# Expert weights as plain float32, two half arrays for up to 64 tokens, and a longer ring of loads

## The chip, the cores and the metric

One core of one Trainium2 chip runs the kernel. The metric is the device time of one execution in microseconds (us), the median of several runs. In what follows PE is the matrix engine, DVE VectorE, ACT ScalarE, POOL GpSimd, and SP the engine whose queue issues the loads of weights.

## The reference

Two decoder layers over 256 tokens of 1024 channels. Each layer has a mixer (sparse attention, a convolution and a state space layer), then a feed-forward part, then a gate with a per-layer embedding, each followed by a layer norm. The feed-forward part of the first layer is dense; that of the second is the one which this change touches:

```python
def moe_swiglu(x, router, w1, w3, w2):
    logits = (x @ router).astype(jnp.float32)
    top_vals, top_idx = lax.top_k(logits, TOP_K)
    wts = jax.nn.softmax(top_vals, axis=-1)
    comb = jnp.einsum('blk,blke->ble', wts, jax.nn.one_hot(top_idx, N_EXPERTS, dtype=jnp.float32))
    y = jnp.zeros(x.shape, jnp.float32)
    for e in range(N_EXPERTS):
        y = y + comb[..., e:e + 1] * swiglu(x, w1[e], w3[e], w2[e])
    return y.astype(x.dtype)
```

There are 8 experts, each token goes to 2 of them, and an expert's weights are 1024x3584 (w1 and w3) and 3584x1024 (w2) in float32: 44 MB an expert, 352 MB in all. With the inputs that the reference draws, the experts get 64, 20, 68, 41, 119, 126, 13 and 61 tokens.

## The kernel before, in words

The layers run one after the other. In the expert stage (`moe`) the experts go in order, 0 to 7. For every pair of experts `gather` takes the tokens' rows by a product with a one-hot matrix (`Dm`, token by slot) into x transposed, 128 slots an expert. `expert` then streams the weights in 42 loads of 1 MB: 28 of w1 and w3 by chunks of 1024, 1024, 1024 and 512 columns (of each chunk first w1's 4 loads, or 2 in the last, then w3's), 14 of w2. The products of w1 and w3 with x (`mgu`, two PSUM banks each) go through SwiGLU into `hb`, `hb` is transposed by PE (`hT`) into `ht`, and `ht` times w2 gives `mo`. `mo` goes back to the tokens by a product with the one-hot matrix transposed (`sc`, the scatter), and DVE adds it to the running sum.

No product is made in plain float32. Every load is split: ACT rounds it to the float32r format (`whi`, line 308) and DVE forms the rest (`wlo`, line 309), in pieces of 128x1024; x and `ht` are split alike. `mm3` (lines 303 to 305) then makes three products for each row of 128 weights and each half of 512 columns: x high times w high, x low times w high, x high times w low.

The loads go into a ring of places (`self.ring`, `load`): 12 for each round, and two more beside them in the first one. SP issues them in order; a load waits until the place's former contents have been split. Two first loads of expert 0 are split ahead (`EARLY`, `ready`). The order of the work on each engine is that of the code as the scheduler of the language lays it out, with `after` holding an instruction behind another one.

An expert may have more than 128 tokens. For that, ahead of expert 6 (`OVF`) all engines read the largest count, and a branch (`tc.If`, line 1457) leads to a second pass or over it; with these inputs it leads over it. The next loads of expert 6 are issued before it, into the places that the second pass doesn't use.

At the end of the last expert the last rows of w2 go by half (`held`), the norm follows, and then the gate's weights, which are loaded through the same ring (four loads of 1 MB).

Of the kernel before, what the change touches and what calls it, by code (L numbers as in the profile page):

```python
# [15 lines left out]
P = 128  # L16
# [14 lines left out]
# columns of the constant table  # L31
# [8 lines left out]
# columns of the per-layer parameter table  # L40
# [10 lines left out]
def const_table():  # L51
    """Constants that depend on shapes alone."""
# [19 lines left out]
def square_consts():  # L72
    """Identity, causal mask, strict order, ones, column numbers."""
    import numpy as np

    r = np.arange(P)
    c = (np.eye(P), np.where(r[None, :] <= r[:, None], 0.0, NEG), (r[:, None] < r[None, :]) * 1.0, np.ones((P, P)), np.broadcast_to(r, (P, P)))
    return np.concatenate(c, 1).astype(np.float32)


def param_table(a):
    """The small parameters of each layer side by side, one row per partition; only moved, never computed on."""
# [3 lines left out]
    for l in range(DEPTH):  # L86
        put = lambda n, v: t[l].__setitem__((slice(None), slice(_L[n], _L[n] + v.shape[1])), v)
        col = lambda v: v.reshape(-1, P).T
        # S5: partition (r, n) of tile j is state n of group 2 j + r
# [19 lines left out]
        w2 = a["cmp_w2"][l].reshape(2, 2, P, 64).transpose(0, 2, 1, 3)  # [j, p, c, d]  # L109
# [7 lines left out]
def lay_out(a):  # L117
    """Arrays in the order in which the kernel reads them."""
# [31 lines left out]
# GpSimd's share: row tiles of a square weight, score tiles that it scales and S5 products, by layer  # L150
# [3 lines left out]
RB = 4  # loads of weights in flight  # L154
RBN = 2  # more of them beside the experts
OV = 2  # the last of them, the overflow's
HB = 4  # split weights in flight
SPARE = ("h1", "h2")  # tiles that take a load before their first use
EARLY = 2  # loads of the first expert split ahead
# [16 lines left out]
GT0 = ("o", "y", "bu", "s")  # L176


# [10 lines left out]
class Trunk:  # L189
    def __init__(self, ctx, tc, a, out):  # L190
# [8 lines left out]
        self.spare = []  # room for loads once the ring is full for the first time  # L199
        self.pre = []  # weights loaded ahead  # L200
        self.ready = []  # weights split ahead
# [12 lines left out]
    def psum(self, name, **tags):  # L214
        """PSUM of a phase: buffers of each kind of tile, acc of two banks, one and tr of one."""
# [27 lines left out]
    def load(self, src, a, b):  # L243
        """DRAM view [128, a, b] -> SBUF."""
        if self.spare and self.nload == self.full:
            pool, tag, n = self.spare.pop(0)
        else:
            pool, tag, n = self.ring[self.nload % len(self.ring)]
            self.nload += 1
        raw = pool.tile([P, 2048], F32, tag=tag, name="wraw", bufs=n)[:, : a * b]  # L250
        v = raw.rearrange("p (a b) -> p a b", a=a)
        self.loaded = self.nc.sync.dma_start(v, src)
        return v

    def parts(self, raw, a, b, low=None):
        """(index, hi, lo) of the a rows of a loaded weight, split into float32r parts; low: the engine of the low parts."""
        nc = self.nc
        step = max(1, 1024 // b)
        for i0 in range(0, a, step):
# [3 lines left out]
            hi = self.st.tile([P, 1024], F32R, tag="hi", name="whi", bufs=HB)[:, :n]  # L263
            lo = self.st.tile([P, 1024], F32R, tag="lo", name="wlo", bufs=HB)[:, :n]
# [5 lines left out]
    def stream(self, src, a, b):  # L270
        if self.ready:
            yield from self.ready.pop(0)
        else:
# [1335 lines left out]
```

## Time and profile before

| | |
|---|---|
| median of 3 runs | 1678.53 us (1678.34 to 1679.22) |
| span of the profiled execution | 1677.6 us, 0.9 below the median |
| busy: PE, DVE, ACT, POOL | 93%, 84%, 66%, 16% |
| moved by DMA | 445.21 MB, mean 265 GB/s |
| expert loads | 336 of 1024 KB |
| expert stage, first to last product | 622.7 to 1628.1 us |

A busy share is that of the whole span, over stages with different limits. PEclk in a row of windows is the clock that PE was granted, as a share of full speed. A timeline row gives the start, the time to the end of the last of its instructions, and how many they are; in brackets stands the idle time before it and who ended it.

### The profile page before, as it was taken

What the parts mean: (1) busy time and instruction counts of PE and PEld (TensorE: products, weight loads), DVE (VectorE), ACT (ScalarE), POOL (GpSimd) and SP (SyncE); (2) the same over time, 40 slices, a digit from 0 to 9 for tenths busy, and PEclk for the clock granted to TensorE, in tenths of its full rate; (3) what the DMA queues carried; (4) which work ended last, traced back from release to release, by engine and by line L of the source; (5) the groups of instructions that cost most, each with busy time, mean ns of one, the idle gap of its engine ahead of it and who ended that gap; (6) DMA issues with size and microseconds to landing.
All of it is one profiled execution on the core that took longest, in us unless ns stands there. A gap on an engine that the chain in (4) does not pass through costs nothing.

```text
span 1677.6 us, 20721 instructions
## 1 busy us (share of the span) xinstructions
PE 1552.2 (93%) x7390; PEld 1235.8 (74%) x7391; DVE 1407.4 (84%) x1635; ACT 1100.2 (66%) x1413; POOL 276.2 (16%) x209
## 2 busy tenths in 40 slices
PE   6676999998988779999999999999999979999997
PEld 6444787886855578878888778778778768878875
DVE  7998567648789679999988988988988978999988
ACT  6355554434655438878877777777777757877874
POOL 5754108303145240000000000000000000010022
PEclk9898999999978779999999999999999989999998
DMA  7421565554540368999989989989989869999941
GB/s 265 151 101 38 196 201 176 176 181 146 178 176 1 137 265 314 361 352 370 361 314 361 360 335 365 356 309 368 349 340 368 331 252 391 384 377 340 365 155 51
DMA packets 139632, 445.21 MB, mean 265 GB/s; under 512 B 7408, under 2 KB 19312, under 8 KB 138496
## 3 DMA queue, kind: packets, MB, share of 16 engines
q1 hardware_dynamic: 138496, 437.42, 71.0%
q0 software_dynamic: 1024, 6.38, 1.0%
q8 instruction: 60, 0.98, 0.2%
q14 instruction: 52, 0.43, 0.1%
HBM read 442.72 MB, written 1.05 MB: 265 GB/s over the span
## 4 chain that ended last, share of the span: by engine, by line
PE 61%; DVE 4%; issue 1%; DMA 1%; ACT 0%; SPq 0%; POOL 0%; DVEq 0%; POOLq 0%; ACTq 0%
PE mgu L305 12%; PE mgu L303 12%; PE mgu L304 12%; PE mo L303 6%; PE mo L304 6%; PE mo L305 6%; PE hT L1405 1%; PE xe L1373 1%; DVE wlo L309 1%; DMA wraw<-in_moe_w_dram 1%; DVE x L526 1%; DVE x L1443 1%; DVE x L527 0%; PE wo L303 0%; PE wo L304 0%
## 5 line engine op out<-in xcount | busy, mean ns | idle before, releaser
L309 DVE TENSOR_TENSOR wlo<-wraw,whi 128x1024 fp32r<-128x1024 f32 (+2 forms) x774 | 930.9, 1231 | 134.5 <-ACT whi L308 101.2
L308 ACT ACTIVATE whi<-wraw 128x1024 fp32r<-128x1024 f32 (+2 forms) x781 | 805.7, 1052 | 257.8 <-PE mgu L304 79.1
L304 PE MATMUL mgu<-whi,xl 128*128 128x512 f32 x896 | 352.6, 394 | 0.0
L303 PE MATMUL mgu<-whi,xh 128*128 128x512 f32 x896 | 352.4, 394 | 0.0
L305 PE MATMUL mgu<-wlo,xh 128*128 128x512 f32 x896 | 339.8, 396 | 5.1 <-DVE wlo L309 5.1
L305 PEld LDWEIGHTS mgu<-wlo,xh 128*128 128x128 f32 x896 | 167.4, 188 | 47.2 <-DVE wlo L309 12.3
L304 PEld LDWEIGHTS mgu<-whi,xl 128*128 128x128 f32 x896 | 168.4, 188 | 36.3 <-DVE xl L309 0.2
L303 PEld LDWEIGHTS mgu<-whi,xh 128*128 128x128 f32 x896 | 168.2, 188 | 35.0
L303 PE MATMUL mo<-whi,ht 128*128 128x512 f32 x448 | 175.9, 393 | 0.0
L304 PE MATMUL mo<-whi,ht 128*128 128x512 f32 x448 | 175.4, 392 | 0.0
L305 PE MATMUL mo<-wlo,ht 128*128 128x512 f32 x448 | 158.2, 392 | 0.1
L505 POOL DMA_DIRECT2D lnp<-in_lnp_dram x5 | 2.8, 567 | 795.9 <-ACT xh L308 766.4
L305 PEld LDWEIGHTS mo<-wlo,ht 128*128 128x128 f32 x448 | 83.8, 188 | 18.9 <-DVE wlo L309 0.5
L304 PEld LDWEIGHTS mo<-whi,ht 128*128 128x128 f32 x448 | 84.1, 188 | 18.2
L303 PEld LDWEIGHTS mo<-whi,ht 128*128 128x128 f32 x448 | 84.2, 188 | 17.7 <-ACT whi L308 0.2
L304 PE MATMUL fffn_w<-whi,xl 128*128 128x512 f32 (+1 forms) x192 | 72.0, 375 | 0.0
L303 PE MATMUL fffn_w<-whi,xh 128*128 128x512 f32 (+1 forms) x192 | 71.7, 373 | 0.0
L305 PE MATMUL fffn_w<-wlo,xh 128*128 128x512 f32 (+1 forms) x192 | 71.5, 372 | 0.0
L308 ACT ACTIVATE ht<-hT 128x512 fp32r<-128x512 f32 x56 | 33.5, 598 | 49.6 <-PE hT L1405 49.5
L1402 DVE TENSOR_TENSOR hb<-hb,mgu 128x512 f32<-128x512 f32 x56 | 38.3, 683 | 25.6 <-PE mgu L305 25.6
L950 DVE SCALAR_TENSOR_TENSOR cy<-upad,pk,cy 128x256 f32<-128x256 f32 x60 | 52.8, 879 | 1.2
L1401 ACT ACTIVATE hb<-mgu 128x512 f32<-128x512 f32 x56 | 33.1, 590 | 13.7 <-PE mgu L305 13.7
(374 smaller groups left out, 2314.0 us busy)
## 6 DMA issues: line engine op xcount, KB each, us to landing
wraw<-in_moe_w_dram SPq DMA_DIRECT2D x336, 1024.0 KB, 5.9
wraw<-in_ffn_w_dram SPq DMA_DIRECT2D x33, 1024.0 KB, 5.1
wraw<-in_cmp_w_dram SPq DMA_DIRECT2D x8, 1024.0 KB, 5.5
wraw<-in_w_out_dram SPq DMA_DIRECT2D x8, 1024.0 KB, 7.6
wraw<-in_ple_gate_w_dram SPq DMA_DIRECT2D x8, 1024.0 KB, 4.9
wraw<-in_w_in_dram SPq DMA_DIRECT2D x8, 792.0 KB, 6.2
wraw<-in_w_in_dram SPq DMA_DIRECT2D x8, 768.0 KB, 8.2
lnp<-in_lnp_dram POOLq DMA_DIRECT2D x5, 1024.0 KB, 4.9
```

Of the source, the lines that this page charges most:

```text
L303: mm(dst, xh, wh, start=start, stop=False)
L304: mm(dst, xl, wh, start=False, stop=False)
L305: return mm(dst, xh, wl, start=False, stop=stop)
L308: h = self.hi = self.nc.scalar.activation(dh, src, AF.Copy)
L309: return h, (low or self.nc.vector).tensor_tensor(dl, src, dh.bitcast(F32), op=ALU.subtract)
L526: nc.vector.scalar_tensor_tensor(out[:, c], r[:, c], mv[:, 0:1], lnp[:, 0, c], op0=ALU.subtract, op1=ALU.mult)
L950: nc.vector.scalar_tensor_tensor(y0, u(0, k), w(0, k), y0, op0=ALU.mult, op1=ALU.add)
L1373: self.gmm = self.nc.tensor.matmul(ps[:, at : at + n], src[:, tt, k * P : (k + 1) * P], Dm[tt], start=first, stop=last)
L1401: nc.scalar.activation(hb, accs[0][h], AF.Silu)
L1402: self.gated = nc.vector.tensor_mul(hb, hb, accs[1][h])
L1405: nc.tensor.transpose(ps[:, i * P : (i + 1) * P], hb[:, i * P : (i + 1) * P], self.ident)
L1443: nc.vector.scalar_tensor_tensor(y[:, tt, hs], sc[h], comb[tt], y[:, tt, hs], op0=ALU.mult, op1=ALU.add)
```

## The change

In the expert stage the weights go to PE as they land, as float32 moving operands, with no split; x and the hidden tile are float32 too. Each row of weights takes two products, one for each half of the columns, in place of six. `either` makes two versions of each group of two loads (`GRP`), 8 products of 512 columns or 16 of 256, and PE picks one by the expert's count, which it reads into a register: with more than 64 tokens (`SM`) the two products go one after the other over the full array (128 slots); with up to 64, the stationary operand has 64 columns, and the two halves of the weights' columns go to the two halves of the array's columns (rows 0 to 63 and 64 to 127 of PSUM, in two banks). The rows of a bank that such a product doesn't write are zeroed first (`pair`, DVE). A second one-hot matrix (`D2`) has the slots 64 further for experts with few tokens, for the scatter of the second half.

The transposes of the hidden tile, of the one-hot matrices and the scatter are put off behind the next group of products (`todo`, `flush`); the gather of the next pair goes into w2's products of the expert before it (`ahead`), but for expert 6, where it follows the overflow. The ring takes in the places of the split weights (`hl`, now one tile for both parts) and of x's low part (`xl`), and one more (`mp`'s); outside of the expert stage the weights are still split. Ahead of the overflow 16 loads of expert 6 are issued. `held`, the last rows by half, is gone. The overflow's second pass uses the full array and has no branch in it.

```diff
@@ the ring, in rest and moe
             if l % 2:
                 self.ring = [(rb, "raw", RBN)] * RBN + [(self.st, "raw", RB)] * RB + [(self.xp, "pp", 1), (ra, "raw", 1)]
-                self.ring += [(re, "raw", 2)] * 2 + [(rd, "raw", OV)] * OV
+                self.ring += [(self.st, "hl", HB)] * HB + [(self.cp, "xl", 1)]
+                self.ring += [(re, "raw", 2)] * 2
...
+                self.over = (rd, "raw", OV)
+                self.ring += [self.over] * OV
...
+        self.ring.append((mp, "raw", 1))
+        self.pre = [self.load(*s) for s in self.expert_loads(j, 0)[:EARLY]]
@@ gather
                 if k % 2 and tt == TORD[1]:
-                    ks = slice(k - 1, k + 1)
-                    self.split(self.xh[:, ks, :n], self.xl[:, ks, :n], ps[:, : 2 * n].rearrange("p (k s) -> p k s", k=2))
+                    v = ps[:, : 2 * n].rearrange("p (k s) -> p k s", k=2)
+                    if k % 4 == 1:
+                        nc.scalar.activation(xe[:, k - 1 : k + 1, :n], v, AF.Copy)
+                    else:
+                        nc.vector.tensor_copy(xe[:, k - 1 : k + 1, :n], v)
@@ expert
+    def either(self, n, emit):
+        if n is None:
+            emit(False)
+        else:
+            with self.tc.If(n > SM) as many:
+                emit(False)
+            with many.Else():
+                emit(True)
+        self.flush()
...
+        rows = (slice(0, SM), slice(P - SM, P))
+        def pair(name):
+            acc = self.pair(name)
+            if n is not None:
+                for h in range(2):
+                    nc.vector.memset(acc[h][rows[1 - h]], 0.0)
+            return acc
...
-                    for kk, wh, wl in self.stream(w[wi][:, u * ku : (u + 1) * ku, c0 : c0 + cw], ku, cw):
-                        k = u * ku + kk
-                        for h in range(cw // 512):
-                            hs = slice(h * 512, (h + 1) * 512)
-                            self.mm3(acc[h], xeh[:, k], xel[:, k], wh[:, hs], wl[:, hs], k == 0, k == KT - 1)
+                    ws = get()
+                    def emit(few):
+                        for u, w in enumerate(ws):
+                            for i in range(ku):
+                                k = (u0 + u) * ku + i
+                                for h in range(2):
+                                    wk = w[:, i, h * hw : (h + 1) * hw]
+                                    dst, x = (acc[h][rows[h], :hw], xe[:, k, 0:SM]) if few else (acc[h][:, :hw], xe[:, k])
+                                    mm(dst, x, wk, start=k == 0, stop=k == KT - 1)
+                    self.either(n, emit)
...
+            self.todo.append(lambda ci=ci, hw=hw, hbs=hbs: turn(ci, hw, hbs))
```

On PE, where the first expert passes from w1 and w3 to w2, the rows before are these (`hT` are transposes, `ht` the hidden tile's parts; the number behind a name tells a tile from the next of its kind):

```order
L305 MATMUL mgu_5558<-wlo_5595,xh_4565 128x512
L303 MATMUL mo_5615<-whi_5619,ht_5084 128x512
L304 MATMUL mo_5615<-whi_5619,ht_5084 128x512
L305 MATMUL mo_5615<-wlo_5620,ht_5084 128x512
L303 MATMUL mo_5616<-whi_5619,ht_5084 128x512
L304 MATMUL mo_5616<-whi_5619,ht_5084 128x512
L305 MATMUL mo_5616<-wlo_5620,ht_5084 128x512
L303 MATMUL mo_5615<-whi_5629,ht_5084 128x512
L1405 MATMUL hT_5608<-sqr_104,hb_5605 128x128 x4
L304 MATMUL mo_5615<-whi_5629,ht_5084 128x512
```

At the same place now, with a pair of branches around each group:

```order
L1444 MATMUL hT<-sqr,hb 128x128 x8
L1412 COMPARE_AND_BRANCH
L1468 MATMUL mgu<-wraw,xe 128x256 x16
L1412 UNCONDITIONAL_BRANCH
L1468 MATMUL mgu<-wraw,xe 64x256 x16
L1412 UNCONDITIONAL_BRANCH
L1444 MATMUL hT<-sqr,hb 128x128 x2
L1412 COMPARE_AND_BRANCH
L1503 MATMUL mo<-wraw,ht 128x512 x8
L1412 UNCONDITIONAL_BRANCH
L1503 MATMUL mo<-wraw,ht 64x512 x8
L1412 UNCONDITIONAL_BRANCH
```

One group of two loads has 24 products before, and has 8 now, in two versions of which one runs; the transposes stand between groups.

On DVE, in the later half of the first expert, before (`wlo` are the low parts of the weights):

```order
L1402 TENSOR_TENSOR hb_5291<-hb_5291,mgu_5200 128x512
L309 TENSOR_TENSOR wlo_5338<-wraw_5335,whi_5337 128x1024
L309 TENSOR_TENSOR wlo_5348<-wraw_5335,whi_5347 128x1024
L309 TENSOR_TENSOR ht_5290<-hT_5294,ht_5290 128x512
L1402 TENSOR_TENSOR hb_5301<-hb_5301,mgu_5201 128x512
L309 TENSOR_TENSOR wlo_5360<-wraw_5357,whi_5359 128x1024
L309 TENSOR_TENSOR wlo_5370<-wraw_5357,whi_5369 128x1024
L309 TENSOR_TENSOR ht_5290<-hT_5304,ht_5290 128x512
L309 TENSOR_TENSOR wlo_5382<-wraw_5379,whi_5381 128x1024
L309 TENSOR_TENSOR wlo_5392<-wraw_5379,whi_5391 128x1024
```

In the same stretch now (`mgu` and `mo` memsets zero the rows of the other half; the branches are jumps to the join that PE's branch needs):

```order
L1476 TENSOR_TENSOR hb<-hb,mgu 128x512
L1412 UNCONDITIONAL_BRANCH
L1476 TENSOR_TENSOR hb<-hb,mgu 128x512
L1432 MEMSET mo 64x512 x2
L1447 COPY ht<-hT 128x512
L1432 MEMSET mgu 64x512
L1412 UNCONDITIONAL_BRANCH
L1432 MEMSET mgu 64x512
L1476 TENSOR_TENSOR hb<-hb,mgu 128x256 x2
L1412 UNCONDITIONAL_BRANCH
L1447 COPY ht<-hT 128x256
L1412 UNCONDITIONAL_BRANCH x7
```

The splits are gone; memsets, copies and unconditional branches stand in their place.

## Rows read from the trace of the kernel before

**Rows 1.** Page, parts 1 (busy us and share) and 4 (the last chain).
```profile
PE 1552.2 (93%) x7390; PEld 1235.8 (74%) x7391; DVE 1407.4 (84%) x1635; ACT 1100.2 (66%) x1413; POOL 276.2 (16%) x209
...
PE 61%; DVE 4%; issue 1%; DMA 1%; ACT 0%; SPq 0%; POOL 0%; DVEq 0%; POOLq 0%; ACTq 0%
```

**Rows 2.** Timeline of PE: start us, us, engine, line, operation.
```profile
699.36 0.39 PE L304 MATMUL mgu<-whi,xl 128*128 128x512 f32 x1
...
700.73 0.39 PE L304 MATMUL mgu<-whi,xl 128*128 128x512 f32 x1
```

**Rows 3.** Timeline: first product of experts 0, 2, 3, 6; last one.
```profile
622.74 0.48 PE L303 MATMUL mgu<-whi,xh 128*128 128x512 f32 x1
...
870.03 0.62 PE L303 MATMUL mgu<-whi,xh 128*128 128x512 f32 x2
...
992.57 0.40 PE L303 MATMUL mgu<-whi,xh 128*128 128x512 f32 x1
...
1386.92 0.63 PE L303 MATMUL mgu<-whi,xh 128*128 128x512 f32 x2
...
1628.12 0.39 PE L305 MATMUL mo<-wlo,ht 128*128 128x512 f32 x1
```

**Rows 4.** Groups by form, 650 to 1600 us: busy us, mean ns.
```profile
L309 DVE TENSOR_TENSOR wlo<-wraw,whi 128x1024 fp32r<-128x1024 f32 x634 | 754.7, 1223 | 48.2 <-ACT whi L308 17.7
```

**Rows 5.** Waits of the load queue, 700 to 1360: us, times, longest.
```profile
SPq L252 <- DVE wlo L309: 550.9, 211, 16.2
```

**Rows 6.** Windows: busy of PE, PEld, DVE, ACT, POOL; PEclk, share, GB/s.
```profile
600.00:610.00 10.00, 2.83 (x21) 2.37 (x19) 9.72 (x8) 2.19 (x4) 8.82 (x4) 0.68 1.01 403
700.00:740.00 40.00, 40.00 (x178) 32.73 (x178) 36.19 (x32) 31.18 (x31) 0.00 (x0) 1.00 1.00 377
1390.00:1440.00 50.00, 50.00 (x229) 40.86 (x228) 46.52 (x44) 40.77 (x45) 0.00 (x0) 1.00 1.03 404
```

**Rows 7.** Timeline of PE: float32 products of 512 columns, full array.
```profile
95.84 1.02 PE L903 MATMUL s<-kTz,qT 128*128 128x512 f32 x2
...
98.66 0.59 PE L903 MATMUL s<-kTz,qT 128*128 128x512 f32 x1
...
L903 PE MATMUL s<-kTz,qT 128*128 128x512 f32 x32 | 19.5, 699 | 2.6 <-ACT kTz L705 2.6
```

**Rows 8.** Timeline of PE: float32 products on two halves of the array.
```profile
529.42 1.09 PE L927 MATMUL o<-pT,vv 128*64 128x128 f32 x16
...
L927 PE MATMUL o<-pT,vv x160: 272/273/687, 101.6 to 576.0; 128*64 128x128 f32 x128, 128*64 128x256 f32 x32
```

**Rows 9.** Instructions of line 1457, the overflow's If: ns minimum, median, maximum.
```profile
L1457 ACTq COMPARE_BRANCH  x1: 50/50/50, 1370.3 to 1370.3; - x1
L1457 PEldq COMPARE_BRANCH  x1: 6032/6032/6032, 1372.2 to 1372.2; - x1
L1457 DVEq COMPARE_BRANCH  x1: 72/72/72, 1373.3 to 1373.3; - x1
```

**Rows 10.** Timeline of the load queue, 550 to 630 us, and parts.
```profile
552.83 75.67 SPq L252 DMA_DIRECT2D wraw<-in_moe_w_dram  x17
...
597.96 2.50 SPq L252 DMA_DIRECT2D wraw<-in_moe_w_dram  x4
...
610.19 2.91 SPq L252 DMA_DIRECT2D wraw<-in_moe_w_dram  x5
```

**Rows 11.** Timeline of PE around the stop before expert 6.
```profile
1371.79 0.63 PE L1441 MATMUL sc<-ot,DT 128*128 128x512 f32 x2
1380.44 0.55 PE L1373 MATMUL xe<-Dm,th 128*128 128x256 f32 x1 [8.03 <-DVE Dm L1252]
```

**Rows 12.** Timeline of the load queue: the gate's loads.
```profile
1622.43 4.14 SPq L252 DMA_DIRECT2D wraw<-in_ple_gate_w_dram  x4
```

**Rows 13.** Windows, as in rows 6, of two stretches of 5 us.
```profile
150.00:155.00 5.00, 2.37 (x18) 1.52 (x18) 5.00 (x9) 1.68 (x3) 3.11 (x3) 1.00 0.06 22
555.00:560.00 5.00, 3.90 (x10) 1.64 (x9) 5.00 (x11) 0.91 (x2) 2.54 (x2) 0.50 0.44 177
```

More of the change, by code (lines that the diff above doesn't have):

```diff
@@ L154 @@
 RB = 4
+EARLY = 8
 RBN = 2
@@ L243, in load, with room, turned @@
     def load(self, src, a, b):
[L245 to L251, printed above, removed]
+        v = self.room(F32, "wraw")[:, : a * b].rearrange("p (a b) -> p a b", a=a)
         self.loaded = self.nc.sync.dma_start(v, src)
         return v
+    def room(self, dt, name):
+        pool, tag, n = self.ring[self.nload % len(self.ring)]
+        self.nload += 1
+        return pool.tile([P, 2048], dt, tag=tag, name=name, bufs=n)
+    def turned(self, *less):
+        n = self.nload % len(self.ring)
+        return [r for r in self.ring[n:] + self.ring[:n] if r[:2] not in less]
     def parts(self, raw, a, b, low=None):
@@ L1100, in ple_late @@
         n = 2 * S
-        self.ring = [r for r in self.ring if r[0] is not self.xp]
+        self.ring, self.nload = self.turned((self.xp, "pp")), 0
         self.pp = self.xp.tile([P, TT, D], F32, tag="pp", name="pp")
@@ L1315, in moe, with pair @@
         normed = []
+        def pair(e):
+            advance(self.gather(th, tl, [one_hot(e, tt) for tt in range(TT)], S, GT))
         for e in range(NE):
             if e == OVF:
-                ring = self.ring
-                n = len(ring) - ring.count(ring[-1])
-                self.nload = 0
-                first = [(c, nm, u) for c in (0, 1024) for nm in ("moe_w1", "moe_w3") for u in range(4)][:n]
-                pre = [self.load(w3d(nm, e)[:, 2 * u : 2 * u + 2, c : c + 1024], 2, 1024) for c, nm, u in first]
@@ L1327, in moe @@
+                pair(e)
             Dm = Da[:, e // 2 % 2]
[L1328 to L1346 removed]
@@ L1347, in moe @@
             es = ts(e % 2)
-            w = [w3d(nm, e) for nm in ("moe_w1", "moe_w3", "moe_w2")]
             De = [Dm[:, tt, e % 2] for tt in range(TT)]
+            D2 = mp.tile([P, TT, P], F32, tag="D2", name="D2")
+            for tt in range(TT):
+                nc.vector.tensor_scalar(D2[:, tt], slots, rank2[:, tt, e : e + 1], sel[:, tt, e : e + 1], op0=ALU.is_equal, op1=ALU.mult)
             ce = [comb[:, tt, e : e + 1] for tt in range(TT)]
-            with self.after(self.dml) if e == 0 else ExitStack():
-                self.expert(mp, w, xh[:, :, es], xl[:, :, es], De, ce, y, norm if e == NE - 1 else None)
+            n = nc.tensor.value_load(cint[0:1, e + 1 : e + 2], min_val=0, max_val=S)
@@ L1353, in moe @@
+            ahead = (lambda: pair(e + 1)) if e % 2 and e + 1 not in (OVF, NE) else None
+            last = e == NE - 1
+            self.expert(mp, self.expert_loads(j, e), n, self.xh[:, :, es], De, [D2[:, tt] for tt in range(TT)], ce, y, ahead, norm if last else None)
             if e == NE - 2:
@@ new lines, in either, with expert, turn @@
+    def either(self, n, emit):
[6 more added lines that the diff above has]
+                emit(True)
+        self.flush()
+    def expert(self, mp, loads, n, xe, Dm, D2, comb, y, ahead=None, done=None):
+        nc = self.nc
+        mm = nc.tensor.matmul
+        loads = iter(loads)
+        get = lambda: [self.pre.pop(0) if (s := next(loads)) and self.pre else self.load(*s) for _ in range(GRP)]
+        rows = (slice(0, SM), slice(P - SM, P))
[5 more added lines that the diff above has]
+            return acc
+        hts = []
+        def turn(ci, hw, hbs):
+            nb = hw // P
+            ht = mp.tile([P, 2 * nb, P], F32, tag=f"h{ci}", name="ht", bufs=1)
+            for h in range(2):
+                ps = self.tr("hT")
+                for i in range(nb):
+                    nc.tensor.transpose(ps[:, i * P : (i + 1) * P], hbs[h][:, i * P : (i + 1) * P], self.ident)
+                dst = ht[:, h * nb : (h + 1) * nb].rearrange("p k t -> p (k t)")
+                if h:
+                    nc.vector.tensor_copy(dst, ps[:, :hw])
+                else:
+                    nc.scalar.activation(dst, ps[:, :hw], AF.Copy)
+                hts.extend((ht[:, h * nb + i], h) for i in range(nb))
+        DT = []
+        for ci, (c0, cw) in enumerate(CHUNKS):
+            hw, ku = cw // 2, 2048 // cw
@@ new lines, in expert, with emit @@
+        acc = pair("mo")
+        NK = D_FFE // P
+        for g in range(0, NK // 2, GRP):
+            ws = get()
+            def emit(few):
+                for u, w in enumerate(ws):
+                    for i in range(2):
+                        k = 2 * (g + u) + i
+                        ht, hf = hts[k]
+                        for h in range(2):
+                            dst, x = (acc[h][rows[h]], ht[:, rows[hf]]) if few else (acc[h], ht)
+                            mm(dst, x, w[:, i, h * 512 : (h + 1) * 512], start=k == 0, stop=k == NK - 1)
+            self.either(n, emit)
+            if g == GRP and ahead:
+                ahead()
@@ new lines, in expert, with scatter @@
+        ots = []
+        for h in range(2):
+            ot = mp.tile([P, 2, 512], F32R, tag=f"h{h}", name="ot", bufs=1)
+            self.split(ot[:, 0], ot[:, 1], acc[h])
+            ots.append(ot)
+        def scatter():
+            normed = ()
+            if done:
+                self.ring, self.nload = self.turned((self.cp, "xl")), 0
+                self.new_xT()
+            for tt in range(TT):
+                sc = self.pair("sc")
+                for h in range(2):
+                    hs = slice(h * 512, (h + 1) * 512)
+                    mm(sc[h], DT[0][:, h, tt], ots[h][:, 0], start=True, stop=False)
+                    mm(sc[h], DT[0][:, h, tt], ots[h][:, 1], start=False, stop=True)
+                    with self.after(*normed):
+                        nc.vector.scalar_tensor_tensor(y[:, tt, hs], sc[h], comb[tt], y[:, tt, hs], op0=ALU.mult, op1=ALU.add)
+                if done:
+                    normed = done(tt)[1:]
@@ L1453, in overflow @@
+        if n is None or done:
+            scatter()
+        else:
+            self.todo.append(scatter)
     def overflow(self, j, mp, Dm, cint, th, tl, rank, sel, comb, y):
@@ L1456, in overflow @@
         most = nc.values_load(cint[0:1, 0:1], min_val=0, max_val=S)
-        with tc.If(most > P):
+        with tc.If(most > P, preferred_fallthrough_block=False):
             num = mp.tile([P, 1], F32, name="num")
```

174 lines of the change are left out of this document (70 added, 104 removed).

## The prediction

> **What bounds the kernel now.** I read the page first: the matrix engine is busy for 93% of the span, and the chain that ended last lies on it for 61%; DMA has 1% of that chain [rows 1]. Nearly all of this is the expert stage, so I went there. A stretch of plain timeline shows its beat: six products of 512 columns from 699.36 to 700.73, 0.228 us each, with no gap [rows 2]. An expert has 84 rows of weights, two halves and three products a row, so 504 x 0.228 = 114.9 us. The first products of the experts stand 122.5 us apart for expert 2 (870.03 to 992.57) and the last product of the stage is at 1628.12, so the stage takes 1005.4 us from 622.74 [rows 3]. The 7.6 us beyond the products are transposes of the hidden tile and the scatter.
>
> The other engines follow this beat. VectorE's part of a load (wlo, 1.22 us, twice a load) fits in the 2.74 us that PE takes for it (12 products of 0.228) [rows 4]. The load queue waits for the place that a wlo frees: 550.9 us over 660 us [rows 5]. DMA moves 377 GB/s in the middle of the stage, and 404 GB/s after the stop before expert 6, where many places come free at once; 403 GB/s also at 600 to 610 us, when it fills the ring [rows 6]. So DMA is second, and close: a load of 1,048,576 B takes 2.60 us at 404 GB/s, against 2.74 us of PE.
>
> **Price of the new products.** Each row has two products in place of six, in plain float32. The nearest row: L903 with 512 columns, float32, full array. The code has 16 of them (two layers, two branches, four heads of one token tile) and the trace 32 records, so a product is two records, and the pair shown ends 1.02 us after it began where one record of it lasts 0.59: 0.43 us apart [rows 7]. An expert with more than 64 tokens costs 168 x 2 x 0.43 = 144 us, more than the 114.9 of now. With up to 64 tokens, two products go to the two halves of the array. L927 is two such halves with 64 columns each and different moving operands: 16 records of 128 columns took 1.09 us, of which the last one's own 0.27 are a tail, so 0.82 / 15 = 0.055 us a record, half of the 0.107 us that 128 columns take at L903's rate [rows 7, 8]. So the halves run side by side, and such an expert costs 72 us. The reference's counts are 64, 20, 68, 41, 119, 126, 13, 61: five experts at 72, three at 144.
>
> The rest of an expert's PE time: the transposes and the scatter stay (7.6), two more transposes of slots, a gather for every second expert (32 products of 256 columns, 3.7 us at half of 0.228), 21 branches. The branches of ACT and DVE at the overflow took 0.05 and 0.07 us [rows 9]; 21 of these are 1.4 us. I take +8 for all, with ends 4 (much of it overlaps) and 12. PE alone: 80 and 152.
>
> What the splits leave: DVE loses about 84 x 1.22 us an expert, ACT as many splits. The new zeroing (18 of 64x512 an expert) cannot pass 18 x 1.22 = 22 us of DVE [rows 4], and DVE has 80: hidden. Copies in place of splits at the gather are shorter than what they replace. Transposes and scatter are now queued behind the next group (3.4 us or more), so PE does not wait for SwiGLU.
>
> **The sum.** Loads now wait for PE alone. Before 597.96 us the queue has issued 7 of the experts' loads (17 in all in this stretch, less 4, 5 and one behind) [rows 10]; I let DMA run through from 601, with the 18 places that the lists of the ring add up to (2, 4, 1, 1, 4, 1, 2, 2 and 1).
> - Expert 0 (64): 622.7 + 80 = 703.
> - Expert 1 (20): PE could end at 783, but load 84 lands at 601 + 77 x 2.60 = 801.2, and its group takes 3.8: 805. DMA-bound, 22 us lost.
> - Expert 2 (68) 957. In 152 us DMA lands 58 loads where 42 are used, so the ring is full. Expert 3 (41): 18 in store and 31 landing cover 42: 1037. Experts 4 and 5: 1189, 1341.
> - The stop before expert 6 stays: from the last scatter at 1371.79 to the first product at 1386.92, 15 us [rows 11], hidden by nothing: 1356. Sixteen loads precede it, two places more are free.
> - Experts 6 and 7 (13, 61): the first group frees places at 1360; 66 loads x 2.60 = 171.6, an estimated 3 for the first to come through, 3.8 for the last group: 1538. PE alone would end at 1516, so DMA bounds again.
>
> The last product was at 1628.1, so -90. The tail takes 2 more (0 to 5): the gate's four loads are issued from 1622.4 now, 6 us ahead of the last product [rows 12]; in a bound DMA they would land up to 4 x 2.6 us after the last expert load, with the gate's splits behind them. Also the last rows no longer go half by half. So -88 against the profiled 1677.6, 1590; the median lies 0.9 above that span: **1591 us**.
>
> Bounds. Load 2.50 us (the 16 engines not quite full at 404): 143 exposed loads x 0.1 = -14, 1577. Load 2.78 (377 GB/s, a lower bound, since places were awaited there): +26, 1617. PE overhead 4 or 12 an expert: experts 2 to 5 alone show it, -/+16, 1575 or 1607.
>
> **Rivals.**
> *DMA holds less.* For it: 377 GB/s over 40 us, at full engine share [rows 6]. Against: that stretch waits for places, and 50 us hold 404. At 2.78 us: 1617. The Trainium skill, "DMA: Bandwidth & Descriptors", section "Where 436 GB/s comes from", says that for moves from HBM about 358 GB/s per core binds. By that a load takes 2.93 us, 143 x 0.33 = 47 us more and some 15 us for expert 3, whose store would run dry: 1653. The trace disagrees in the two stretches of 403 and 404 [rows 6]; the page's section "Bandwidth" gives 425 for a core alone.
>
> *Slower: the branches.* This is the other side. PE alone would need 5 x 80 + 3 x 152 + 15 = 871 us where it takes 1005 now, so 134 us are there for 168 branches, and from 0.80 us each the kernel is slower. The place is PE's sequencer at every group: it reads a count, jumps over one arm and back. For it: PE's one taken branch in the trace, over the overflow's body, took 6.03 us [rows 9], and PE stood 8.03 us [rows 11]. If one in four paid that, 253 us: PE would end at 1747, 1800 in all. Against: the arms are 32 instructions, the overflow's body over a thousand, and other engines' jumps took 0.05 to 0.07; a full matrix queue hides what is short. Half of the break-even, 0.4 us each, is 8.4 an expert, in the four experts where PE is the bound: 1625. The Trainium skill, "Runtime: NRT & Kernel Launch", section "Instruction fetch mechanics", says that a branch out of the two pages at hand (256 instructions each) stalls for a fetch. The trace's 6.03 us agrees for the far jump; by the rule these jumps mostly stay within, though both arms must be fetched.
>
> *The halves do not overlap* in this shape: few = 152, all experts 8 x 152 + 15 = 1231 us, end 1854: 1907. L927 speaks against it [rows 8].
>
> *The clock falls* where PE waits for DMA. For it: 555 to 560, PE 3.90 of 5 us busy at 0.50, the 1.2 GHz level; against: 150 to 155, 2.37 of 5 us busy at 1.00 [rows 13]. In experts 0, 1, 6, 7 PE is to be busy some 70 to 75%. Cold, a few-expert takes 152: experts 0 and 1 end 122 later, 6 and 7 at 1356 + 122 + 304 = 1782: 1835.
>
> *Nothing happens*: needs PE to lose exactly what it gains.
>
> **Chances and range.** Forecast, within 1575 to 1610: 0.58. DMA slower, 1610 to 1655: 0.12. Branches of 0.3 to 0.7 us, 1612 to 1670: 0.08. Under 1575 (overhead hidden, 2.50): 0.07. No change: 0.02. Slower: branches 0.07, halves 0.03, clock 0.03. The range 1565 to 1650 leaves out about 0.2: most of the slower cases and some of each end. By 0.2% of the time, 3 us, about what a measurement can tell from no change: faster 0.85, same 0.02, slower 0.13.
>
> **What the new profile would show.** Right: PE records 0.43 us apart for experts 2, 4, 5, and pairs in 0.43 for the others; few-experts 80 us apart where the ring is full (expert 3) and about 105 at the start; the load queue never waiting on DVE in the stage; 400 GB/s and more up to 805 and from 1360; a clock of 1.00. Wrong: expert 3 near 100 us with idle PE behind branches (rival 2), expert 1's loads landing 2.8 us or more apart, pairs in 0.86 us, or a clock of 0.50. I would be most wrong if PE's sequencer, and not its array, set the time of the few-experts.

## The result, and the profile after

The changed kernel took 1608.06 us (1606.63 to 1610.99, 4 runs) against 1678.43 us of the kernel before in the same runs: a ratio of 0.9587, 95% interval 0.9574 to 0.9601. That is 70 us less, where the forecast was 87 less (1591 us) and the range 1565 to 1650. The profiled execution has a span of 1608.8 us; it is the longest of the four (1610.99), and a profile shows one execution only, so the places of rows of two profiles can differ by a few us where the medians do not.

The first products of the experts, and the last group, in the timeline of PE; they answer to [rows 3] (the last of the eight records of the last row begins at 1547.44):

```profile
622.48 1.08 PE L1468 MATMUL mgu<-wraw,xe 128*64 128x512 f32 x4
...
700.76 1.46 PE L1468 MATMUL mgu<-wraw,xe 128*64 128x512 f32 x6
...
808.91 1.10 PE L1468 MATMUL mgu<-wraw,xe 128*128 128x512 f32 x2 [0.70 <-ACT ot L313]
...
959.54 0.65 PE L1468 MATMUL mgu<-wraw,xe 128*64 128x512 f32 x2
...
1046.58 0.70 PE L1468 MATMUL mgu<-wraw,xe 128*128 128x512 f32 x1
...
1198.08 0.59 PE L1468 MATMUL mgu<-wraw,xe 128*128 128x512 f32 x1
...
1349.42 0.50 PE L1523 MATMUL sc<-ot,DT 128*128 128x512 f32 x1
...
1363.22 1.08 PE L1468 MATMUL mgu<-wraw,xe 128*64 128x512 f32 x4
...
1546.09 1.94 PE L1503 MATMUL mo<-wraw,ht 128*64 128x512 f32 x8 [0.66 <-DMA wraw<-in_moe_w_dram]
```

Read against the sum of the prediction, with the starts of products throughout:

| | forecast | measured |
|---|---|---|
| expert 0 ends (64 tokens) | 703 | 700.8 |
| expert 1 ends (20) | 805 | 808.9 |
| expert 2 ends (68) | 957 | 959.5 |
| expert 3 ends (41) | 1037 | 1046.6 |
| expert 4 ends (119) | 1189 | 1198.1 |
| expert 5 ends (126) | 1341 | 1349.4 |
| expert 6 begins | 1356 | 1363.2 |
| last product of the stage | 1538 | 1547.4 |
| from there to the end | 51.5 | 61.4 |

So the stage took 925 us where it took 1005, and about half of what the forecast missed lies behind the stage. Page, parts 1, 4 and 6 (busy; the last chain by engine; loads, with the median time from issue to landing):

```profile
PE 1454.2 (90%) x6318; PEld 832.5 (52%) x6319; DVE 678.0 (42%) x1105; ACT 401.3 (25%) x719; POOL 266.0 (17%) x205
...
PE 8%; DMA 6%; DVE 1%; issue 0%; ACT 0%; POOL 0%; SPq 0%; DVEq 0%; POOLq 0%
...
wraw<-in_moe_w_dram SPq DMA_DIRECT2D x336, 1024.0 KB, 17.5
```

DVE is busy for 42% in place of 84%, ACT for 25% in place of 66% [rows 1]. The chain that ended last no longer lies on PE for 61%: in it DMA has 6% and PE 8%, the rest is not resolved, and I read no bound from it. The loads' median of 17.5 us from issue to landing stood at 5.9 before: at one load in 2.6 us, some seven are under way at a time now (an estimate, 17.5 / 2.6). The queue of loads, 700 to 1340 us, answers to [rows 5]:

```profile
SPq L249 <- PE mgu L1468: 243.1, 111, 7.0
SPq L249 <- PE mo L1503: 145.2, 52, 11.4
```

It waits for PE to give places back, never for DVE. Windows (busy of PE, PEld, DVE, ACT and POOL; PEclk, DMA share, GB/s), the first of them ahead of the stage, say which bound holds where:

```profile
600.00:610.00 10.00, 7.87 (x64) 7.61 (x63) 6.80 (x18) 0.94 (x3) 1.42 (x1) 0.90 0.68 245
700.00:760.00 60.00, 50.31 (x220) 16.33 (x218) 15.75 (x30) 6.13 (x11) 0.00 (x0) 1.00 1.03 407
960.00:1046.00 86.00, 83.68 (x438) 36.86 (x436) 21.79 (x42) 8.07 (x16) 0.00 (x0) 1.00 1.02 393
1200.00:1350.00 150.00, 148.94 (x405) 73.55 (x403) 19.07 (x35) 7.88 (x15) 0.00 (x0) 1.00 0.84 278
1350.00:1370.00 20.00, 15.34 (x71) 9.81 (x73) 8.34 (x16) 1.42 (x3) 0.60 (x1) 0.83 0.69 249
1370.00:1380.00 10.00, 10.00 (x48) 3.30 (x46) 0.00 (x0) 1.08 (x2) 0.00 (x0) 1.00 0.73 271
1450.00:1500.00 50.00, 41.92 (x184) 13.63 (x180) 9.58 (x19) 5.05 (x9) 0.00 (x0) 1.00 1.03 407
```

In experts 1 and 7 (700 to 760, 1450 to 1500) DMA moves 407 GB/s with its engines full, and PE is idle for a sixth of the time. In experts 3 and 5 PE is busy for 97 to 99%; in expert 5 DMA falls to 278 GB/s, since the ring is full. The clock is at 1.00 in both kinds. Around the stop (1350 to 1370) neither is full: PE is busy for 77% and the granted clock has a mean of 0.83. From 1370 to 1380 PE is busy throughout, from the store, while DMA is still at 271 GB/s. The new products, by form, 650 to 1545 us (busy us, mean ns of one | idle before):

```profile
L1468 PE MATMUL mgu<-wraw,xe 128*128 128x512 f32 x576 | 249.8, 593 | 2.0 <-ACT ot L313 0.7 <-ACT hb L1475 0.7 <-DVE mgu L1432 0.6
L1468 PE MATMUL mgu<-wraw,xe 128*64 128x512 f32 x844 | 194.1, 597 | 18.8 <-DMA wraw<-in_moe_w_dram 13.4 <-DVE mgu L1432 2.4 <-DVE hb L1476 1.4
...
L1432 DVE MEMSET mgu<- 64x512 f32 x117 | 56.7, 485 | 88.8 <-ACT hb L1475 74.3 <-DVE mgu L1432 5.1 <-issue 4.1
```

576 records of the full array in 249.8 us are 0.434 us each; 844 of the halves in 194.1 are 0.230, a pair in 0.46, waits apart but the ends of groups included. Within a group the rows above show it more closely: two records of the full array take 1.10 us (808.91) and four of the halves 1.08 (622.48), so a pair of halves takes the time of one record, 0.43 us from start to start in either case. What the 0.46 holds beyond that lies at the ends of groups: from the last product of a group to the next transpose's start are 0.523 us behind halves and 0.429 behind the full array, and from a transpose to the next product 0.203 and 0.109. A change between halves and full array thus costs 0.094 us, and expert 0 has 12 of them, 1.1 us. The zeroing costs 0.485 us each, 57 us in all on DVE, which is idle more than that; PE waited for it 2.9 us in all ahead of products of w1 and w3. PE's branches, of line 1412 (ns minimum, median, maximum), stand beside [rows 9]:

```profile
L1412 PEldq COMPARE_BRANCH  x231: 65/202/367, 621.3 to 1540.9; - x116
```

The overflow's, of line 1539, in the same columns:

```profile
L1539 PEldq COMPARE_BRANCH  x2: 71/1978/3885, 1351.4 to 1352.8; - x2
```

A branch of a group takes PE's sequencer 0.2 us at the median, some three to four times what the other engines' branches took in [rows 9]; the longer of the overflow's two took 3.9 us.

### The profile page after: what moved, and what is told of

It reads as the page before. It is cut to its first block, busy times and chain, and to the rows that moved or that the text cites. A ratio compares the mean times of both kernels' runs of the same rounds, so it can differ in the third digit from the quotient of the medians.

```text
span 1608.8 us, 16526 instructions
## 1 busy us (share of the span) xinstructions
PE 1454.2 (90%) x6318; PEld 832.5 (52%) x6319; DVE 678.0 (42%) x1105; ACT 401.3 (25%) x719; POOL 266.0 (17%) x205
## 5 line engine op out<-in xcount | busy, mean ns | idle before, releaser
L1468 PE MATMUL mgu<-wraw,xe 128*64 128x512 f32 (+3 forms) x2048 | 548.5, 542 | 25.4 <-DMA wraw<-in_moe_w_dram 17.3
L1468 PEld LDWEIGHTS mgu<-wraw,xe 128*64 128x64 f32 (+1 forms) x2048 | 238.3, 157 | 318.4 <-issue 246.9
L1503 PE MATMUL mo<-wraw,ht 128*64 128x512 f32 (+1 forms) x896 | 272.0, 595 | 12.4 <-DMA wraw<-in_moe_w_dram 12.4
L1503 PEld LDWEIGHTS mo<-wraw,ht 128*64 128x64 f32 (+1 forms) x896 | 101.0, 157 | 172.0 <-issue 143.1
L314 DVE TENSOR_TENSOR whl<-wraw,whl 128x1024 fp32r<-128x1024 f32 (+2 forms) x106 | 136.5, 1297 | 81.7 <-ACT whl L313 81.1
L313 ACT ACTIVATE whl<-wraw 128x1024 fp32r<-128x1024 f32 (+3 forms) x109 | 107.5, 994 | 138.3 <-PE fffn_w L310 44.6
L1432 DVE MEMSET mgu<- 64x512 f32 x128 | 62.1, 485 | 100.2 <-ACT hb L1475 84.1
L310 PE MATMUL fffn_w<-whl,xh 128*128 128x512 f32 (+1 forms) x192 | 71.8, 374 | 0.0
L309 PE MATMUL fffn_w<-whl,xl 128*128 128x512 f32 (+1 forms) x192 | 71.7, 373 | 0.0
L308 PE MATMUL fffn_w<-whl,xh 128*128 128x512 f32 (+1 forms) x192 | 71.4, 372 | 0.0
L308 PEld LDWEIGHTS fffn_w<-whl,xh 128*128 128x128 f32 x192 | 36.1, 188 | 6.7
L310 PEld LDWEIGHTS fffn_w<-whl,xh 128*128 128x128 f32 x192 | 36.1, 188 | 6.2
## 6 DMA issues: line engine op xcount, KB each, us to landing
wraw<-in_moe_w_dram SPq DMA_DIRECT2D x336, 1024.0 KB, 17.5
```

The source lines that it names most:

```text
L308: mm(dst, xh, wh, start=start, stop=False)
L309: mm(dst, xl, wh, start=False, stop=False)
L310: return mm(dst, xh, wl, start=False, stop=stop)
L313: h = self.hi = self.nc.scalar.activation(dh, src, AF.Copy)
L314: return h, (low or self.nc.vector).tensor_tensor(dl, src, dh.bitcast(F32), op=ALU.subtract)
L1432: nc.vector.memset(acc[h][rows[1 - h]], 0.0)
```

## Experiments

Theory: DMA at 2.60 us a load sets the end of experts 0 and 1 together, and of 6 and 7 together (experts 0 and 6 run at PE's own 78 us from the store, and what PE gains there it waits for in the next one); PE's array, at 0.43 us a record or a pair of them, is the bound in experts 2 to 5; the branches cost next to nothing; the tail grew since the gate's loads come last. Rivals: the branches or the doubled program cost PE time; the gain is that of the missing splits or of the ring alone; the tail grew for a reason of its own. All ratios are to the kernel before; the change itself is at 0.9587.

| run | time, us | ratio, 95% interval | expert 2 begins | expert 6 begins | last product | tail |
|---|---|---|---|---|---|---|
| the change | 1608.06 | 0.9587 (0.9574 to 0.9601) | 808.9 | 1363.2 | 1547.4 | 61.4 |
| fixed arms | 1602.27 | 0.9543 (0.9522 to 0.9563) | 807.0 | 1361.3 | 1541.0 | 60.9 |
| full array for all | 1897.19 | one run | 919.5 | 1541.8 | 1840.0 | 55.0 |
| ring of 12 | 1633.67 | 0.9739 (0.9719 to 0.9759) | 818.0 | 1375.9 | 1573.3 | 57.4 |
| loads alone | 1527.26 | one run | 806.1 | 1255.4 | 1464.4 | 61.1 |
| groups of one load | 1631.11 | 0.9713 (0.9686 to 0.9739) | 809.0 | 1382.8 | 1570.2 | 61.2 |
| stop ahead of expert 7 | 1608.66 | 0.9585 (0.9566 to 0.9604) | 803.7 | 1348.6 | 1539.1 | 65.7 |
| stop ahead of expert 1 | 1606.85 | 0.9575 (0.9557 to 0.9592) | 812.8 | 1357.1 | 1538.0 | 64.7 |
| gate first | 1612.66 | 0.9603 (0.9581 to 0.9624) | 807.4 | 1361.8 | 1556.0 | 56.2 |
| places of the tail | 1604.29 | 0.9554 (0.9536 to 0.9573) | 808.4 | 1362.1 | 1546.3 | 57.5 |
| projection early | 1616.84 | 0.9635 (0.9615 to 0.9654) | 805.5 | 1360.1 | 1561.8 | 51.6 |
| projection early, stop ahead of 1 | 1611.30 | 0.9594 (0.9575 to 0.9612) | 813.2 | 1357.5 | 1558.0 | 52.0 |
| stop ahead of 1, places of the tail | 1597.68 | 0.9522 (0.9509 to 0.9535) | 812.0 | 1356.3 | 1538.5 | 57.3 |

(The first product of the stage lies between 616.6 and 622.5 in these profiles.)

**Full array for all.** Half of the change alone: unsplit float32 weights and the longer ring, with no half arrays.

```diff
-        nc.vector.tensor_scalar(cnt, cnt, float(SM), float(P - SM), op0=ALU.is_le, op1=ALU.mult)
+        nc.vector.tensor_scalar(cnt, cnt, 0.0, float(P - SM), op0=ALU.is_le, op1=ALU.mult)
...
-            with self.tc.If(n > SM) as many:
+            with self.tc.If(n > 0) as many:
```

> Every expert takes the arm of the full array: the weights are unsplit float32, but no expert uses half arrays (the branches stay). If the half arrays run side by side and are what pays, every expert takes 150 to 152 us, PE is the bound throughout, the stage ends at about 622 + 8 x 151 + 14 = 1844, the load queue is never short, and the time is 1890 to 1905, well over the 1678 of the kernel before. If the gain were that of the missing splits or of the longer ring, the time would stay under 1678.

Measured: 1897.19 us, 219 slower than before, as the theory has it; experts take 148 to 156 us. Without the half arrays the change loses: two float32 products (four records of 0.43 us) cost more than six of float32r (0.228 each [rows 2]), and the splits that went were off the path. All of the gain, and more, is that of the five experts with up to 64 tokens.

**Loads alone.**

```diff
-                            for i in range(ku):
+                            for i in range(1):
...
-                                    mm(dst, x, wk, start=k == 0, stop=k == KT - 1)
+                                    mm(dst, x, wk, start=k == 0, stop=k == KT - ku)
...
-                    for i in range(2):
+                    for i in range(1):
...
-                            mm(dst, x, w[:, i, h * 512 : (h + 1) * 512], start=k == 0, stop=k == NK - 1)
+                            mm(dst, x, w[:, i, h * 512 : (h + 1) * 512], start=k == 0, stop=k == NK - 2)
```

> All loads stay, but of each load only one row of two (or of four) goes into products, so the products are incomplete; PE needs at most half its time and never bounds. If DMA is the second bound at 2.60 us a load, loads 8 to 336 land from about 600 to 600 + 329 x 2.60 = 1455, plus some 10 us at the stop, and the stage ends near 1468, 80 us ahead of the change, at 400 GB/s and more throughout. If DMA can't hold this for 800 us (2.78 us a load at 377 GB/s, 2.93 at 358), it ends at 1525 or at 1575.

Measured: the last product at 1464.4 (1468 expected), 107 to 110 us for each of experts 1 to 4, 2.6 us a load. Windows of this run:

```profile
700.00:800.00 100.00, 68.45 (x231) 20.14 (x229) 19.71 (x39) 8.01 (x15) 0.00 (x0) 0.76 1.03 407
900.00:1000.00 100.00, 70.05 (x229) 21.32 (x229) 22.15 (x42) 9.20 (x17) 0.00 (x0) 0.82 1.03 407
1300.00:1400.00 100.00, 66.24 (x207) 16.25 (x205) 19.35 (x35) 8.29 (x16) 5.37 (x5) 0.75 1.03 406
```

407 GB/s over 100 us at a time: this is what DMA holds, and the 377 GB/s of the kernel before [rows 6] was what PE asked for. The slower rates of the rival are out. The Trainium skill, "DMA: Bandwidth & Descriptors", section "Where 436 GB/s comes from", states that for moves from HBM the HBM side, about 358 GB/s a core, binds. This trace differs, with 407, and the measurement decides.

**Fixed arms.**

```diff
-            n = nc.tensor.value_load(cint[0:1, e + 1 : e + 2], min_val=0, max_val=S)
+            n = (64, 20, 68, 41, 119, 126, 13, 61)[e]
...
-            with self.tc.If(n > SM) as many:
-                emit(False)
-            with many.Else():
-                emit(True)
+            emit(n <= SM)
```

> The arms are fixed when the kernel is built, by these inputs' counts: no count is read and no branch taken in the groups, and only one arm is in the program; nothing else changes. If the time of a group is the array's (0.43 us for a record of 512 columns, or for a pair of them), at most 0.1 us a group goes in experts 2 to 5, the only ones in which PE is the bound: 84 x 0.1 = 8 us at the most, 1600 to 1608, and expert 4 stays within 3 us of its 151.5 us. If the branches or the doubled program cost PE 0.2 us a group or more, expert 4 falls under 147 us and the time under 1592.

Measured: 1602.27 us, 6 less; the intervals of the ratios do not overlap (the gap is 0.0011), so it is a gain, and a small one. Expert 4 takes 149.9 us in place of 151.5, 0.08 us a group. Expert 3 took longer (91.7 us for 87.0), and from the start of expert 2 to that of expert 6 both kernels take 554.3 us. So the experts that PE bounds gain nothing in sum, and the rival's 0.2 us a group is out for them. The 6 us lie elsewhere: 1.5 in an earlier first product, and most of the rest behind the stop, where DMA moved more. This is the stretch from 1370 to 1380 us of this run, where the change has 271 GB/s:

```profile
1370.00:1380.00 10.00, 10.00 (x51) 3.75 (x48) 2.84 (x6) 0.59 (x1) 0.00 (x0) 1.00 1.03 415
```

The 144 GB/s between them over 10 us are 1.4 loads, or 3.7 us. How the branches hold loads back there is not shown, and neither is why expert 3 took longer. Counts known beforehand save 6 us of 1608 in all.

**Groups of one load.** `GRP = 2` becomes `GRP = 1`.

> One load a group in place of two: 42 branches an expert in place of 21, with 4 products of 512 columns in an arm, and places come free load by load. If a branch costs nothing that PE's queue doesn't cover, the time stays at 1608 within 5. If it costs 0.2 us or more, experts 2 to 5 grow by 17 us or more in sum, and the time is over 1622.

Measured: 1631.11 us, 23 more. It does not test what it was to test. With smaller groups the order on PE changed: the first four groups of the next expert now stand between the last four groups of w2, as this timeline at the start of expert 4 shows.

```profile
1054.78 3.70 PE L1468 MATMUL mgu<-wraw,xe 128*128 128x512 f32 x8
1058.41 1.94 PE L1503 MATMUL mo<-wraw,ht 128*64 128x512 f32 x8
1060.28 3.70 PE L1468 MATMUL mgu<-wraw,xe 128*128 128x512 f32 x8
1063.91 1.94 PE L1503 MATMUL mo<-wraw,ht 128*64 128x512 f32 x8
```

At the start of expert 2, 798 to 834 us, PE's longest wait (us, times, longest) was this:

```profile
PE mgu L1468 <- DMA wraw<-in_moe_w_dram: 8.4, 1, 8.4
```

PE stood 8.4 us for a load of the next expert while work of the last one was queued behind it. A branch took 0.18 us at the median, no more than in the change. The run is inconclusive on branches.

**Ring of 12.**

```diff
-        self.ring.append((mp, "raw", 1))
...
-                self.ring += [(self.st, "hl", HB)] * HB + [(self.cp, "xl", 1)]
```

> The ring has 12 places in place of 18: those of the split weights, of x's low part and one more are left out of it; products as in the change. If the store of loads carries experts of few tokens behind experts of many, six places less mean six loads of 2.6 us less in hand at the first expert, at expert 3 and behind the stop: 16 us at the end, 5 to 15 at expert 3, 5 to 8 at the start, so 1630 to 1645, with expert 3 at 95 to 100 us. If only the rate of DMA counts, it stays within 5 us of 1608.

Measured: 1633.67 us, 26 more. The last product is 26 us later: expert 6 began 12.7 us later and experts 6 and 7 took 197 us in place of 184, 13 more where six loads of 2.6 were forecast to take 16. Expert 3 took 89.5, less than the 95 to 100 expected; most of the early loss, 13 us, is in expert 0 (91.5 us for 78.3, from a first product 5.5 us earlier). So six places are worth 26 us, a third of the gain. The tail is 4 us shorter (57.4), without the places of the split weights in the ring; the runs on the tail below come back to that.

**The stop.** First ahead of expert 7 (`OVF = 7`, with the next norm's parameters taken behind it), then ahead of expert 1:

```diff
-OVF = 6
+OVF = 1
...
-                pair(e)
+                pair(e & ~1)
...
-            ahead = (lambda: pair(e + 1)) if e % 2 and e + 1 not in (OVF, NE) else None
+            ahead = (lambda: pair(e + 1)) if e % 2 and e + 1 != NE else None
```

> The stop for the overflow goes from ahead of expert 6 to ahead of expert 7, and the pair's gather is made again behind it (32 products); expert 6's gather goes into expert 5. If the end of the stage is DMA's (66 loads behind the last free places), the stop costs nothing there as long as loads go on: expert 6's loads follow expert 5's without a halt, 14 us go, and 3 to 5 come back since the load queue waits at the stop until what it issued has landed: 1597 to 1600. If PE bounds the end, or the load queue's wait at the stop costs more than the stop itself, the time is 1606 or above.

> The stop for the overflow goes from ahead of expert 6 to ahead of expert 1, where PE waits for DMA anyway (28 us in expert 1 as the change ran); the pair's gather is made again behind it. If the stop's price is PE's 14 us and the 11 us of DMA that the load queue loses while it waits for its loads, PE's part is covered here: expert 2 begins 4 to 8 us later (the load queue's wait), expert 6 begins 6 to 10 us earlier, the stage ends 8 to 14 us earlier, 1594 to 1600. If the load queue loses more here than the stop cost (all loads of expert 1 depend on it), the time is 1606 or above.

Measured: 1608.66 and 1606.85, neither apart from the change by their intervals. In the first the last product is 8 us earlier, 5 of them from an earlier first product, and the tail is 4 longer. DMA pays for the stop in another place, as a window behind the stop in expert 7 of the first run shows, beside the ten microseconds in which PE is busy for 4:

```profile
1430.00:1440.00 10.00, 3.99 (x16) 1.63 (x12) 6.25 (x12) 1.09 (x2) 2.02 (x3) 0.96 1.03 409
1460.00:1470.00 10.00, 10.00 (x52) 3.76 (x50) 3.38 (x6) 2.10 (x5) 0.00 (x0) 1.00 0.33 107
```

The same in expert 1 of the second run:

```profile
730.00:740.00 10.00, 9.23 (x48) 3.48 (x44) 5.61 (x12) 2.18 (x4) 0.00 (x0) 1.00 0.34 137
```

At the stop the load queue waits until all that it has issued has landed, and then begins anew (in the second run no load is issued between the one of 717.41 and that of 739.07): 107 and 137 GB/s for 10 us, some 7 us lost. In the second run's profile the stage ended 9 us earlier, 3 of them from an earlier first product, and the tail took 3; by the medians 1 us is left.

**The tail.** Three runs. Gate first: the gate's loads (`ple_load`) ahead of the last six loads of expert 7:

```diff
-        raws = list(self.ple_load(l))
+        raws = self.graws
...
         for g in range(0, NK // 2, GRP):
+            if done and g == 8:
+                self.graws = list(self.ple_load(1))
             ws = get()
```

> The gate's four loads are issued ahead of the last six loads of expert 7 in place of behind them; the bytes are the same. If the tail of 60.8 us (49.5 before) is longer because the gate's weights arrive last, and because loads in flight share the queue's rate, the last product of the stage comes 6 to 10 us later (1554 to 1558), the tail falls to 50 to 53 us, and the sum stays within 4 us of 1608. If the tail is longer for another reason (the last rows that no longer go by half, the places for the split weights), the tail keeps 58 us or more and the time grows by 6 to 10.

Measured: 1612.66 us; the last product 8.6 us later, the tail 5.2 shorter. The bytes moved from the tail to the stage, and the tail kept 6 to 7 us over the 49.5 of before, more than expected: half right. Places of the tail:

```diff
-        self.ring, self.nload = self.turned((self.xp, "pp")), 0
+        self.ring, self.nload = self.turned((self.xp, "pp"), (self.st, "hl")), 0
```

> After the last expert load the places of the split weights are left out of the ring, so no load of the gate waits for the embedding projection's split (GpSimd's part of it frees the place of the last gate load, which is issued at 1558.16 in the change's profile, 10 us behind the last product); nothing else changes. If the longer tail (61.4 us, 49.5 before) is made by gate loads that wait for these places, all four are issued by 1542, the tail falls to 53 to 56 us, and the time to 1600 to 1604. If it is made by the projection's late load and split alone, which PE's queue puts ahead of the norm's transposes, the tail keeps 60 us or more and the time stays within 3 of 1608.

Measured: 1604.29 us, the tail 57.5. The load queue from 1525 us on, first of the change, then of this run:

```profile
1532.24 2.31 SPq L249 DMA_DIRECT2D wraw<-in_ple_gate_w_dram  x1
1534.60 0.46 SPq L249 DMA_DIRECT2D wraw<-in_ple_proj_dram  x1
1535.77 22.76 SPq L249 DMA_DIRECT2D wraw<-in_ple_gate_w_dram  x3
```

```profile
1531.16 2.31 SPq L249 DMA_DIRECT2D wraw<-in_ple_proj_dram  x1
1533.56 8.69 SPq L249 DMA_DIRECT2D wraw<-in_ple_gate_w_dram  x4
```

In the change the gate's last three loads took 22.76 us to issue; here all four took 8.69. The change's load queue waited, from 1500 to 1575 us, for GpSimd's split of the projection's weights and for the projection's load, and neither wait is in this run:

```profile
SPq L249 <- DMA wraw<-in_ple_proj_dram: 9.1, 1, 9.1
SPq L249 <- POOL whl L314: 6.3, 1, 6.3
```

So 4 us of the tail, 11.9 longer than before, were this wait. Projection early:

```diff
                 bias = self.ple_bias(l, mp.tile([P, D], F32, tag="h2", name="gb"), more[:, 0])
-        advance(self.ple_late(l))
+                advance(self.ple_late(l))
```

> The embedding projection (two loads, their split, 24 products on PE) goes between experts 6 and 7 in place of behind expert 7; the stop stays ahead of expert 6. PE waits for DMA there anyway. If the tail is made by what follows the last expert load in the load queue, the last product of the stage comes about 3 us later (1.25 MB more ahead of it), the first product of the gate follows it by 11 to 13 us in place of 18.8, and the time falls by 4 to 6: 1602 to 1604. If the gate's four loads alone make the tail, it stays within 3 of 1608.

Measured: 1616.84 us. The tail fell to 51.6, 2 above that of before. This takes the projection out of the tail, where the kernel before had it too, so its 5.9 us against the run of the places are the projection's whole share, not its growth. The timelines give the growth: the projection's last product begins 9.2 us behind the stage's last before, 18.5 in the change and 15.5 with the places, so 6 of the 12 us fit a projection that ends later even so; this is read from the places, and no run gives the projection its old time back. And the last product came 14 us later, not 3, since the load queue now waited for the projection's products to give places back (DMA fell to 101 and 93 GB/s in the two stretches of 10 us from 1440):

```profile
SPq L249 <- PE pp L310: 28.7, 2, 28.5
```

**Together.**

> The two moves together: the projection between experts 6 and 7, and the stop for the overflow ahead of expert 1. With the stop's 9 us (stage end 1538 in place of 1547 with the stop moved) and the tail's 7 us less 3 for the loads that go ahead: 1596 to 1600. If the tail grows by what the stage gains, as it did when the stop alone was moved, 1603 to 1608.

> The stop ahead of expert 1 and the gate's loads kept out of the places of the split weights, together. With the stop moved alone, the stage ended 9 us earlier and the tail grew by 3, its gate loads issued from 1548.62, 10 us behind the last product. If these waits ate the gain, the tail is 56 to 58 us now behind a stage that ends near 1538, and the time 1596 to 1599. If the tail grows for another reason, the time is 1602 or more.

Measured: 1611.30 us for the projection with the stop, a miss of both ranges for the same reason as above (a wait of 28.2 us for the projection's products). The stop ahead of expert 1 with the places of the tail took 1597.68 us, a ratio of 0.9522 (0.9509 to 0.9535): it beats both kernels, the changed one by 10 us, with the tail at 57.3 behind a stage that ends at 1538.5.

## Why the prediction was right, and where it was off

- *The halves run side by side*: right; read from 16 small products [rows 8], it held for 512 columns, 78.3 us for expert 0 where 80 were forecast. The rival of separate halves is out by the same 78.3, against 148.2 on the full array.
- *0.43 us a record, 152 us for many tokens*: right (150.6 and 151.5 us for experts 2 and 4), and so is the loss in these experts against the 122.5 of before [rows 3].
- *DMA at 2.60 us a load*: right (2.6 in the run of loads alone); experts 6 and 7 took 184 us where 182 were forecast. The lower bound's 2.50 us a load had no row behind it, since at 404 GB/s the engines' share was already 1.03 [rows 6]; the shortest expert in the run of loads alone took 2.55 us a load (107.2 / 42, experts 1 to 4).
- *The clock*: stayed at 1.00 in experts 1 and 7, so the rival did not come true in the change. The fall that it feared exists: in the run of loads alone the clock went to 0.50 again and again (last section). In the change it stands at 0.50 after the stop (1355.5 to 1362.3) and in the tail (1556.8 to 1563.7), where PE had waited before.
- *The branches*: 0.2 us each in the sequencer, nothing in sum in the experts that PE bounds, and 6 us in all by the run without them, most of which come through the loads behind the stop. The slower rival, 0.80 us each, was far off. The overflow's own branch took 3.9 us, not 6.03.
- *Mis-sized terms.* "+8 for all" of an expert's other work is a mean, and expert 3 bears more than it: it took 87.0 us, 15 beyond its products, as the scatter of expert 2, the whole gather of the next pair (from 1013.7 to 1025.9 the gather takes 4.7 us of PE) and a wait of PE for a zeroed bank (1.5 us, which the prediction had as hidden) fall in it; 7 us. Expert 1 ended 4 us later than the sum had it: PE took up its last load at 806.3, where the sum had it land at 801.2, since DMA moved 245 GB/s from 600 to 610 us where the sum let it run through from 601. The tail, "2 more (0 to 5)", grew by 11.9: the step that failed is that the gate's loads follow at 2.6 us each. They waited for places that the projection's split held (4 us), and the projection itself ended later (6, by its place in the timelines). These make 21 us; the rest of the steps gave 2 back, which leaves 19 in the profiled execution, and the median lies 17 above the forecast. The errors nearly all lie on one side, so that the forecast came this near is not luck of errors that cancel.

## What to carry to other kernels

When an edit takes work off engines that wait, its price is set by the engine that doesn't: here the splits were free, and the trade of six fast products for two slow ones pays only through the half arrays. Between two bounds that alternate by stretch, a store of loads carries the one over the other: here six places, 16 us of loads, were worth 13 us up to expert 6 and 13 behind it. Look at what queues behind the stage that gets shorter: its weights now arrive last, and a shared ring can make them wait for their neighbours' places.

## What I had not expected of the hardware

In the run of loads alone the mean granted clock was 0.75 to 0.82 over three stretches of 100 us, while it was 1.00 in experts 1 and 7 of the change. Shorter windows of that run show no level between: the clock goes back and forth between 0.50 (1.2 GHz) and 1.00 (2.4 GHz), while PE, with half its products or more left out, waits for loads.

```profile
701.40:711.40 10.00, 6.33 (x25) 1.77 (x21) 4.49 (x8) 1.09 (x2) 0.00 (x0) 1.00 1.03 408
711.60:721.60 10.00, 8.04 (x21) 2.24 (x21) 2.25 (x4) 0.60 (x1) 0.00 (x0) 0.50 1.02 409
```

It cost that run nothing, since DMA set its pace, with 408 and 409 GB/s at either level. And loads of 1 MB took 17.5 us each to land at the median in the change, where they had taken 5.9, though DMA moved more and not less (a mean of 277 GB/s, 265 before).
